# Where a feed-forward's temporary sums lie, and when the next weight is prepared

## The chip, the cores and the metric

The kernel runs on one core of a Trainium2 chip. The metric is the device time of one execution in microseconds. TensorE (PE) multiplies, ScalarE (ACT) and VectorE (DVE) prepare operands and read results back, GpSimd (POOL) and SyncE (SP) start transfers. Each engine works through its own list of instructions in order, and semaphores hold an instruction until what it needs is there. The lists are fixed when the kernel is built.

## The reference

Two layers of a decoder trunk on 512 tokens of width 1024, in float32. In each layer:

```python
h = rmsnorm(x)
z = h @ w_in                     # queries, keys, values of three token mixers, merge gates
m = sum(sigmoid(gate_b) * (mixer_b(z) @ w_br_b) for b in "abc")   # window, sparse, latent attention
x = x + m @ w_out
x = x + cross_attention(rmsnorm(x), rmsnorm(mem))    # 4 heads on 256 memory tokens, w_xq, w_xkv, w_xo
h = rmsnorm(x)
x = x + (silu(h @ w_gate) * (h @ w_up)) @ w_down     # 22 blocks of 128 hidden features
```

Mixer C is the latent attention: its queries come from a normalised latent of 384 features, by a product without and one with a rotary position, and its keys and values from a normalised latent of 256.

## The kernel before

**Numbers.** A float32 product is made of three matmuls: operand and weight are each split into a high half (a rounding cast on ScalarE) and a low half (the difference, on VectorE), and TensorE adds high x high, high x low, and low x high. In the code these are the matmuls of L307, L308 and L309 of `mm3`, or of L294 of `quads`. L307 and L308 need a weight's high half `wh` and the operand's two halves, L309 the weight's low half `wl`.

**Weights.** They stream through a fixed plan of units of 128 x 1024. `unit` takes the next one for a task. `load` starts its DMA on SyncE's queue (L222, three buffers `wraw`), and `halve` casts it (`wh`, L246, two buffers) and subtracts (`wl`, L166 by a helper). `ahead` loads further and prepares the next unit. `mm3` calls it after the block of 128 rows whose number is its argument `ahead`; with None it doesn't.

**Tiles that share a unit.** Four places use one unit for two tiles of output: the position projection of mixer C (`pe`, weight `w_mpe`, three blocks for each tile), its keys and values (`kv`, `w_mkv`), the merge product (`product`, `w_br`), and the output projection of the cross attention (`out_task`, `w_xo`). There the first tile passes None, and the second prepares the next unit.

**The order.** Tasks are Python generators that run side by side in stages (`skew`). A list scheduler then places each engine's instructions, so that the written order is not the order on an engine.

**The feed-forward.** The 22 pairs of gate and up blocks are computed in two ways. Pairs 0 to 3 are plain: `gate(j)`, `up(j)`. Pairs 4 to 21 use a scheme with seven products in place of eight: `p1` to `p7`, each of 12 matmuls of 256 columns (`quads`), in the order p1(4), p5(4), p2(4), p6(4), p3(4), p1(5), p7(4), p5(5), p2(5), p4(4), p6(5), p3(5), p1(6), p7(5). They need sums of weights and sums of operands.

- Sums of weights: `load_sum` copies the up block into a tile `sum` (tag S31r, two buffers, L262, SyncE) and adds the gate block to it by an accumulating DMA from GpSimd's queue (L266). `halve_sum` makes the halves `S31h` (L172) and `S31l` (L173), and then the tile is read once more for the sum `S24`.
- Sums of operands: `normed` makes the normalised operand `y` in the row form during `gate(1)` and `up(1)`. `sums(0)` follows `gate(2)` and `sums(1)` follows `up(2)`. Each makes four temporaries f[0] to f[3] from quarters of `y` and splits them into the tiles `T`, which the pair tasks read: `trans(i)` hands out T's part i, of which `p5`, `p6`, `p7` and `p4` read 0, 1, 2 and 3. f[1] is made from f[0], f[3] from f[1]. `operand` splits `y` itself into `xh` and `xl` for `p1`, `p2` and `p3`.

Before the change the four temporaries come from `self.tmp()`, a tag of five buffers that evacuated products use as well. The sums of pairs 4 and 5 are both loaded ahead of the feed-forward, since S31r's two buffers are free.

Of the kernel before, what the change touches and what calls it, by code (L numbers as in the profile page):

```python
# [8 lines left out]
F32 = mybir.dt.float32  # L9
# [137 lines left out]
class Trunk:  # L147
# [787 lines left out]
    def pe_tasks(self, l, lq, out):  # L935

        nc, w = self.nc, []

        def pe(t):
            if t == 0:  # L940
                w.append(self.unit("w_mpe", l, nblk=6))
            ps = self.mm()
            yield from self.mm3(ps, w[0], range(3 * t, 3 * t + 3), lq, ahead=1 if t else None)
            yield STAGE
            f, s = self.tmp(), self.tmp()
            nc.scalar.copy(f, ps)
            for q in range(0, 128, 32):
                nc.sync.dma_start(s[q:q + 16], f[q + 16:q + 32])
                nc.sync.dma_start(s[q + 16:q + 32], f[q:q + 16])
            yield STAGE  # L950
            yield 0
            yield STAGE
            r = self.pp.tile([128, 512], F32, name="lf", tag="lf", bufs=5)
            self.tt(s, s, self.spe, OP.mult)
            self.tt(r, f, self.cpe, OP.mult)
            self.tt(r, r, s, OP.add)
            out.append(r)

        return [pe(0), pe(1)]

    def pair_tasks(self, l, p, lq, lkv, pe, box):

        nc, at = self.nc, self.at
        w, fs, ks, vs = [], [], {}, {}

        def kv(g):
            if g == 0:
                w.append(self.unit("w_mkv", l, p, nblk=4))
            ps = self.mm()
            yield from self.mm3(ps, w[0], range(2 * g, 2 + 2 * g), lkv, ahead=0 if g else None)  # L970
            yield STAGE
            f = self.tmp()
            nc.scalar.copy(f, ps)
            yield STAGE
            tp = self.tp4(f)
            yield 430
            k = ks[g] = at.tile([128, 2, 512], F32R, name="k", tag="k", bufs=2)
            for i in range(2):
                nc.sync.dma_start(k[64:96, i].bitcast(F32), self.kpe[64 + 32 * i:96 + 32 * i].bitcast(F32))
            self.split(k[0:64, 0], k[0:64, 1], f[0:64])  # L980
            yield STAGE
            v = vs[g] = at.tile([128, 4, 128], F32R, name="v", tag="v", bufs=2)
            self.split(v[:, :, 64 * g:64 * g + 64], v[:, :, 64 - 64 * g:128 - 64 * g], tp[:, :, 64:128])

        def product():
            ps = yield from self.proj(("w_mq", l, p), lq)
            yield STAGE
            for g in range(2):
                f = self.tmp()
                h = 2 * p + g  # L990
                nc.scalar.copy(f[0:64], ps[64 * g:64 * g + 64])
                nc.scalar.copy(f[64:96], pe[h // 4][32 * (h % 4):32 * (h % 4) + 32])
                fs.append(f)

        def query(g):
            yield 0
            yield STAGE
            q = at.tile([128, 2, 512], F32R, name="q", tag="q", bufs=2)
            self.split(q[0:96, 0], q[0:96, 1], fs[g][0:96])
            yield STAGE  # L1000
            box[2 * p + g] = (q, ks[g], vs[g])

        return [kv(0), kv(1), product(), query(0), query(1)]

    def jobs_c(self, box, of):
# [27 lines left out]
    def merge_tasks(self, l, x, n, br, of, done=None):  # L1033

        nc = self.nc
        os, ts, ws = [], {}, {}

        def halves():
            yield 0
            for f in of:  # L1040
                o = self.mx.tile([128, 2, 512], F32R, name="oh", tag="oh", bufs=4)
                self.split(o[:, 0], o[:, 1], f)
                os.append((o[:, 0], o[:, 1]))
            del of[:]

        def gate(i):
            ps = yield from self.proj(("w_in", l, (T_GA, T_GB, T_GC)[br] + i), x)
            yield STAGE
            f = self.mx.tile([128, 512], F32, name="gt", tag="gt", bufs=2)
            self.evac(ps, n["r"], f)  # L1050
            nc.scalar.activation(f, f, AF.Tanh, scale=0.5)
            ts[i] = f

        def product(i):
            if i % 2 == 0:
                ws[i // 2] = self.unit("w_br", l, br, i // 2)
            w = ws[i // 2]
            b0 = 4 * (i % 2)
            ps = self.mm()
            yield from self.mm3(ps, w, range(b0, b0 + 4), os, ahead=1 if i % 2 else None)  # L1060
            yield STAGE
            t = ts.pop(i)
            if br == 0:
                m = self.mx.tile([128, 512], F32, name="mg", tag="mg", bufs=8)
                self.mg.append(m)
                nc.vector.scalar_tensor_tensor(m, t, 1.0, ps, op0=OP.add, op1=OP.mult)
            else:
                m = self.mg[i]
                nc.vector.scalar_tensor_tensor(t, t, 1.0, ps, op0=OP.add, op1=OP.mult)
                self.tt(m, m, t, OP.add)  # L1070
            if done is not None:
                yield STAGE
                done(m)

        out = [halves()]
        for i in range(0, 8, 2):
            out += [gate(i), gate(i + 1), product(i), product(i + 1)]
        return out
# [143 lines left out]
    def cross(self, l, st, xt, xa, mem):  # L1222
        nc = self.nc
        self.at = xa
        x, n, qs, os = st["x"], {}, {}, {}
# [42 lines left out]
        o = [(os[h][:, 0], os[h][:, 1]) for h in range(4)]  # L1268
        st, n = self.norm_begin(), {}
        ws = {}  # L1270

        def out_task(i):
            if i % 2 == 0:
                ws[i // 2] = self.unit("w_xo", l, i // 2)
            ps = self.mm()
            b0 = 4 * (i % 2)
            yield from self.mm3(ps, ws[i // 2], range(b0, b0 + 4), o, ahead=1 if i % 2 else None)
            yield STAGE
            self.tt(xt[i], xt[i], ps, OP.add)
            self.norm_split(st, xt[i], i, l * G_LAYER + G_FFN)  # L1280
            self.norm_tile(st, xt[i])

        drain(skew([out_task(i) for i in range(KT)]))
        return st, n

    def ffn(self, l, st, n, xt, ff, last):
# [39 lines left out]
        def sums(i):  # L1326

            if i == 0:
                ts.extend([[ff.tile([128, 4, 256], F32R, name="T", tag="T", bufs=8) for _ in "hl"] for _ in range(4)])
            c, f = slice(2 * i, 2 * i + 2), [self.tmp((128, 2, 256)) for _ in range(4)]  # L1330
            b11, b12, b21, b22 = (ys[k][:, :, h] for k in (i, 2 + i) for h in (slice(0, 256), slice(256, 512)))
            self.tt(f[0], b11, b12, OP.subtract)
            self.tt(f[2], b22, b12, OP.subtract)
            nc.vector.scalar_tensor_tensor(f[1], f[0], -1.0, b22, op0=OP.mult, op1=OP.subtract)
            nc.vector.scalar_tensor_tensor(f[3], f[1], -1.0, b21, op0=OP.mult, op1=OP.subtract)
            for t, src in zip(ts, f):
                self.split(t[0][:, c], t[1][:, c], src)
# [89 lines left out]
        def down(i, part):  # L1427
# [4 lines left out]
            if end:  # L1432
                if not last:
# [5 lines left out]
        m = sum(FFN_PARTS) - 1  # L1439
        tasks = [self.norm_end(st, D, n), gate(0), up(0), after(gate(1), (normed, 0), (normed, 2)),  # L1440
                 after(up(1), (normed, 1), (normed, 3)), after(gate(2), (sums, 0)), after(up(2), (sums, 1))]
        tasks += [gate(3), up(3)]
        for j in range(PLAIN, m):
# [12 lines left out]
        ws, sh, rh = {}, [self.norm_begin(256, nc.vector, ff) for _ in range(2)], [{}, {}]  # L1456
# [162 lines left out]
```

## Time and profile before

| | us |
|---|---|
| median of 3 runs | 2002.15 |
| lowest, highest | 2000.5, 2004.52 |
| the profiled execution | 2001.81 |
| its span in the trace | 2000.1 |
| TensorE busy in it | 1965.3 (98%) |
| VectorE busy | 1400.3 (70%) |
| ScalarE busy | 1187.7 (59%) |
| GpSimd busy | 70.1 (4%) |

The span runs from the first to the last instruction on the engines; what lies around it is 1.7 us. TensorE's busy time holds stretches in which several matmuls overlap in the pipeline, so gaps in the row of matmuls are read from the distance between their starts. In the names of the trace the buffer numbers are left out: `wh` is the same as `wh_6838` in the order below.

### The profile page before, as it was taken

What the parts mean: (1) busy time and instruction counts of PE and PEld (TensorE: products, weight loads), DVE (VectorE), ACT (ScalarE), POOL (GpSimd) and SP (SyncE); (2) the same over time, 40 slices, a digit from 0 to 9 for tenths busy, and PEclk for the clock granted to TensorE, in tenths of its full rate; (3) what the DMA queues carried; (4) which work ended last, traced back from release to release, by engine and by line L of the source; (5) the groups of instructions that cost most, each with busy time, mean ns of one, the idle gap of its engine ahead of it and who ended that gap; (6) DMA issues with size and microseconds to landing.
All of it is one profiled execution on the core that took longest, in us unless ns stands there. A gap on an engine that the chain in (4) does not pass through costs nothing.

```text
span 2000.1 us, 30439 instructions
## 1 busy us (share of the span) xinstructions
PE 1965.3 (98%) x11390; PEld 1691.0 (85%) x11390; DVE 1400.3 (70%) x2699; ACT 1187.7 (59%) x2282; POOL 70.1 (4%) x113
## 2 busy tenths in 40 slices
PE   8999999999999999999999999999999999999998
PEld 6878887888888798989878788878888888989898
DVE  7897777676557884847678877676665679657475
ACT  5777776875446552534456867877744566435254
POOL 1000000000000010100001000000000000001000
PEclk9999999999999999999999999999999999999999
DMA  6432212224332473645344322132333344657432
GB/s 193 116 91 60 68 48 82 77 88 139 100 105 87 129 200 116 184 123 137 112 133 110 83 68 59 55 90 74 116 111 106 99 132 114 167 141 196 115 104 73
DMA packets 86764, 220.07 MB, mean 110 GB/s; under 512 B 11208, under 2 KB 17096, under 8 KB 86616
## 3 DMA queue, kind: packets, MB, share of 16 engines
q1 hardware_dynamic: 76680, 199.21, 32.5%
q0 software_dynamic: 9792, 18.88, 5.9%
q8 instruction: 89, 1.46, 0.3%
q14 instruction: 59, 0.48, 0.1%
q10 hardware_dynamic: 144, 0.04, 0.0%
HBM read 200.23 MB, written 4.75 MB: 102 GB/s over the span
## 4 chain that ended last, share of the span: by engine, by line
PE 80%; DVE 8%; ACT 7%; DMA 2%; issue 2%; SPq 0%; POOL 0%; DVEq 0%; ACTq 0%
PE mm L307 17%; PE mm L309 17%; PE mm L308 17%; PE s L294 10%; PE tp L294 5%; PE av L674 3%; PE tp L628 3%; PE av L294 3%; ACT p L614 2%; ACT p L602 1%; DVE wl L166 1%; DMA sum<-in_w_gu 1%; ACT wh L246 1%; DVE p L596 1%; ACT ph L172 1%
## 5 line engine op out<-in xcount | busy, mean ns | idle before, releaser
L246 ACT CAST wh<-wraw 128x1024 fp32r<-128x1024 f32 (+3 forms) x275 | 277.5, 1009 | 397.0 <-PE mm L308 230.0
L307 PE MATMUL mm<-xh,wh 128*128 128x512 f32 x928 | 376.9, 406 | 3.4 <-ACT wh L246 2.0
L309 PE MATMUL mm<-xh,wl 128*128 128x512 f32 x928 | 366.0, 395 | 4.8 <-DVE wl L166 4.7
L166 DVE TENSOR_TENSOR wl<-wraw,wh 128x1024 fp32r<-128x1024 f32 (+3 forms) x275 | 322.7, 1174 | 64.2 <-ACT wh L246 61.2
L308 PE MATMUL mm<-xl,wh 128*128 128x512 f32 x928 | 367.1, 396 | 0.3 <-DVE xl L176 0.3
L309 PEld LDWEIGHTS mm<-xh,wl 128*128 128x128 f32 x928 | 174.8, 188 | 42.9 <-DVE wl L166 6.5
L307 PEld LDWEIGHTS mm<-xh,wh 128*128 128x128 f32 x928 | 175.3, 189 | 34.3 <-ACT wh L246 3.3
L308 PEld LDWEIGHTS mm<-xl,wh 128*128 128x128 f32 x928 | 175.6, 189 | 31.5 <-issue 1.7
L602 ACT ACTIVATE p<-p,st 128x256 f32<-128x256 f32 (+5 forms) x288 | 154.8, 538 | 57.2 <-DVE st L596 53.0
L166 DVE TENSOR_TENSOR x<-x,mm 128x512 f32<-128x512 f32 (+1 forms) x88 | 55.6, 637 | 146.0 <-PE mm L309 145.6
L614 ACT ACTIVATE p<-p,st 128x256 f32<-128x256 f32 (+3 forms) x288 | 139.9, 531 | 25.0 <-DVE st L166 16.5
L173 DVE TENSOR_TENSOR pl<-tp,ph 128x384 fp32r<-128x384 f32 (+1 forms) x192 | 116.7, 610 | 42.5 <-ACT ph L172 41.6
L596 DVE CUSTOM_DVE_ANT_0 p<-s,causal 128x128 f32<-128x128 f32 (+2 forms) x224 | 106.0, 475 | 43.3 <-PE s L1016 21.3
L172 ACT CAST ph<-tp 128x384 fp32r<-128x384 f32 (+1 forms) x192 | 98.7, 517 | 37.1 <-PE tp L628 35.1
L307 PE MATMUL mm<-h,wh 128*128 128x512 f32 x304 | 120.3, 396 | 0.0
L308 PE MATMUL mm<-h,wh 128*128 128x512 f32 x304 | 120.2, 395 | 0.0
L309 PE MATMUL mm<-h,wl 128*128 128x512 f32 x304 | 120.2, 395 | 0.0
L628 PE MATMUL tp<-ident,p 128*128 128x128 f32 x656 | 110.9, 277 | 4.8 <-DVE v L173 2.2
L266 POOL DMA_DIRECT2D sum<-in_w_gu x36 | 43.3, 1213 | 1581.4 <-DVE acc L166 530.5
L628 PEld LDWEIGHTS tp<-ident,p 128*128 128x128 f32 x656 | 75.7, 140 | 22.0 <-ACT p L614 8.3
L307 PE MATMUL mm<-oh,wh 128*128 128x512 f32 x192 | 79.4, 413 | 0.0
L309 PE MATMUL mm<-oh,wl 128*128 128x512 f32 x192 | 76.7, 399 | 0.0
(300 smaller groups left out, 4796.1 us busy)
## 6 DMA issues: line engine op xcount, KB each, us to landing
wraw<-in_w_in SPq DMA_DIRECT2D x91, 512.0 KB, 3.6
wraw<-in_w_gu SPq DMA_DIRECT2D x52, 512.0 KB, 3.7
sum<-in_w_gu SPq DMA_DIRECT2D x36, 512.0 KB, 4.4
sum<-in_w_gu POOLq DMA_DIRECT2D x36, 512.0 KB, 5.8
wraw<-in_w_d SPq DMA_DIRECT2D x32, 512.0 KB, 3.7
wraw<-in_w_br SPq DMA_DIRECT2D x24, 512.0 KB, 3.6
up<-in_w_gu SPq DMA_DIRECT2D x36, 256.0 KB, 3.4
wraw<-in_w_xkv SPq DMA_DIRECT2D x16, 512.0 KB, 3.6
```

What stands on the lines that cost most here:

```text
L166: (eng or self.nc.vector).tensor_tensor(out=out, in0=a, in1=b, op=op)
L172: nc.scalar.copy(hi, src)
L173: (eng or nc.vector).tensor_tensor(out=lo, in0=src, in1=hi.bitcast(F32), op=OP.subtract)
L246: nc.scalar.copy(wh[:, j:j + n], raw[:, j:j + n])
L294: nc.tensor.matmul(ps, a[:, c], b, start=start and i + k == 0, stop=i == 3 and k == 2, skip_group_check=not start)
L307: nc.tensor.matmul(ps, wh[:, c], xh, start=i == 0, stop=False)
L308: nc.tensor.matmul(ps, wh[:, c], xl, start=False, stop=False)
L309: nc.tensor.matmul(ps, wl[:, c], xh, start=False, stop=i == len(blocks) - 1)
L596: o.nc.vector.tensor_tensor_reduce(out=p, in0=self.ps.pop(i), in1=self.mask(self.blocks[i]), scale=-self.scale, scalar=self.init, op0=OP.a ...
L602: self.o.nc.scalar.activation(p, p, AF.Exp, scale=-1.0, bias=st[:, 0, i:i + 1], accum_out=st[:, 1, i:i + 1])
L614: nc.scalar.activation(self.p[j], self.p[j], AF.Copy, scale=self.st[:, 2, j:j + 1])
L628: o.nc.tensor.transpose(tp[:, n], self.p[j][:, c:c + 128], o.ident)
```

## The change

It has two parts. In the four places where two tiles share a unit, the first tile also prepares the next unit, after its block 0 or 1. And in `sums` the four temporaries no longer come from `tmp`, but from two tiles of the tag S31r, f[0] and f[1] in the first, f[2] and f[3] in the second. That tag has two buffers as before, so its tiles now follow each other in this order: the sum of pair 4, the temporaries of `sums(0)` (f_6994, f_6995), the sum of pair 5 (sum_7015), the temporaries of `sums(1)` (f_7056, f_7057), the sum of pair 6 (sum_7127), and so on. A tile can be written only when the last reader of the tile two places ahead of it is done.

```diff
-            yield from self.mm3(ps, w[0], range(3 * t, 3 * t + 3), lq, ahead=1 if t else None)
+            yield from self.mm3(ps, w[0], range(3 * t, 3 * t + 3), lq, ahead=1)
...
-            yield from self.mm3(ps, w[0], range(2 * g, 2 + 2 * g), lkv, ahead=0 if g else None)
+            yield from self.mm3(ps, w[0], range(2 * g, 2 + 2 * g), lkv, ahead=0)
...
-            yield from self.mm3(ps, w, range(b0, b0 + 4), os, ahead=1 if i % 2 else None)
+            yield from self.mm3(ps, w, range(b0, b0 + 4), os, ahead=1)
...
-            yield from self.mm3(ps, ws[i // 2], range(b0, b0 + 4), o, ahead=1 if i % 2 else None)
+            yield from self.mm3(ps, ws[i // 2], range(b0, b0 + 4), o, ahead=1)
...
-            c, f = slice(2 * i, 2 * i + 2), [self.tmp((128, 2, 256)) for _ in range(4)]
+            c, f = slice(2 * i, 2 * i + 2), []
+
+            for _ in range(2):
+                t = ff.tile([128, 2, 2, 256], F32, name="f", tag="S31r", bufs=2)
+                f += [t[:, 0], t[:, 1]]
```

What it does to the order is seen best on ScalarE. The first place is the start of mixer C in layer 0, where the latent `lat` is normalised (`rstd`, `lf`), the first keys and values (`tmp`) are copied out of PSUM, and `wraw_3553` is the unit of the merge product. Before:

```order
L375 COPY rstd_3544<-av_3542 128x512
L973 COPY tmp_3646<-mm_3623 128x512
L973 COPY tmp_3668<-mm_3633 128x512
L175 ACTIVATE lat_3578<-lf_3311,gains_69 128x512
L175 ACTIVATE lat_3582<-lf_3405,gains_69 128x512
L175 ACTIVATE lat_3586<-lf_3410,gains_69 128x512
L172 CAST k_3663<-tmp_3646 64x512
L246 CAST wh_3679<-wraw_3553 128x1024
```

After:

```order
L375 COPY rstd_3544<-av_3542 128x512
L973 COPY tmp_3646<-mm_3623 128x512
L246 CAST wh_3657<-wraw_3553 128x1024
L175 ACTIVATE lat_3578<-lf_3311,gains_69 128x512
L175 ACTIVATE lat_3582<-lf_3405,gains_69 128x512
L175 ACTIVATE lat_3586<-lf_3410,gains_69 128x512
L172 CAST k_3669<-tmp_3646 64x512
L973 COPY tmp_3674<-mm_3639 128x512
```

The cast of the merge product's weight (wh_3679 before, wh_3657 now) has moved from behind the latent to ahead of it, and the second copy from ahead of the latent to behind it. On VectorE the weight's subtraction has likewise moved ahead of the latent's three low halves, and on TensorE four of the eight transposes of the copies have moved behind the matmuls of the position projection. Layer 1 is the same.

The second place is the start of the feed-forward in layer 0: `S31h` are the sums of weights, `dh` a difference block for `p4`, `wh_6838` the weight of `up(1)`. Before:

```order
L364 ACTIVATE sd_6786<-av_6781,eps_71 128x4
L172 CAST S31h_7030<-sum_6956 128x1024
L172 CAST S31h_7159<-sum_7017 128x1024
L172 CAST dh_7192<-up_7020 128x512
L375 COPY rstd_6793<-av_6791 128x512
L246 CAST wh_6838<-wraw_6717 128x1024
L1299 ACT_TABLE_LOAD
L1299 ACTIVATE tmp_6826<-tmp_6826 128x512
```

After:

```order
L364 ACT_TABLE_LOAD
L364 ACTIVATE sd_6786<-av_6781,eps_71 128x4
L172 CAST S31h_7028<-sum_6956 128x1024
L375 COPY rstd_6793<-av_6791 128x512
L1299 ACT_TABLE_LOAD
L1299 ACTIVATE tmp_6826<-tmp_6826 128x512
L246 CAST wh_6838<-wraw_6696 128x1024
```

Only the sum of pair 4 is cast here now; `dh` has gone ahead of these rows, and the weight of `up(1)` stands behind the first SiLU (`tmp_6826`).

The third place is where the operand is split just ahead of the first pair task `p1(4)`. Before:

```order
L172 CAST xh0_6587<-y_6900 128x256
L172 CAST xh1_6607<-y_6900 128x256
L172 CAST xh2_6634<-y_6943 128x256
L172 CAST xh3_6655<-y_6943 128x256
L172 CAST T_6992<-tmp_7061 128x512
L172 CAST xh4_6682<-y_6903 128x512
L172 CAST xh5_6703<-y_6903 128x512
L172 CAST xh6_6730<-y_6946 128x512
L246 CAST wh_7134<-wraw_6959 128x1024
L172 CAST xh7_6738<-y_6946 128x512
```

After:

```order
L172 CAST xh0_6587<-y_6900 128x256
L172 CAST xh1_6613<-y_6900 128x256
L172 CAST S31h_7155<-sum_7015 128x1024
L172 CAST xh2_6634<-y_6943 128x256
L172 CAST xh3_6661<-y_6943 128x256
L172 CAST xh4_6682<-y_6903 128x512
L172 CAST xh5_6709<-y_6903 128x512
L172 CAST xh6_6730<-y_6946 128x512
L246 CAST wh_7130<-wraw_6959 128x1024
L172 CAST xh7_6738<-y_6946 128x512
```

The cast of the sum of pair 5 stands between xh1 and xh2 now. The two casts that made T from the second half's f[2] and f[3], of which `T_6992` stood in these rows, come some ten rows further on, behind the copy `s2` of `p6(4)`; on VectorE f_7057 is made behind the last of the low halves xl and behind the sums that read sum_7015. In SyncE's queue sum_7015 stands behind the unit `wraw_6959`, and sum_7127 two units further on.

## Rows read from the trace of the kernel before

Times are us from the start of the span.

**Rows 1.** The page: busy time of the engines, and the TensorE clock in 40 slices.

```profile
PE 1965.3 (98%) x11390; PEld 1691.0 (85%) x11390; DVE 1400.3 (70%) x2699; ACT 1187.7 (59%) x2282; POOL 70.1 (4%) x113
...
PEclk9999999999999999999999999999999999999999
```

**Rows 2.** TensorE's waits: us in total, times, longest us.

```profile
PE mm L309 <- DVE wl L166: 4.7, 3, 1.7
PE tp L530 <- ACT tmp L973: 2.3, 2, 1.2
```

**Rows 3.** TensorE timeline, layer 0, FFN start: start us, us, instruction, [idle, releaser].

```profile
667.71 0.39 PE L309 MATMUL mm<-xh,wl 128*128 128x512 f32 x1
669.32 0.49 PE L307 MATMUL mm<-xh,wh 128*128 128x512 f32 x1 [1.22 <-ACT wh L246]
669.65 0.40 PE L308 MATMUL mm<-xl,wh 128*128 128x512 f32 x1
671.56 0.50 PE L309 MATMUL mm<-xh,wl 128*128 128x512 f32 x1 [1.51 <-DVE wl L166]
```

**Rows 4.** The same of layer 1.

```profile
1654.57 0.40 PE L308 MATMUL mm<-xl,wh 128*128 128x512 f32 x1
1656.47 0.50 PE L309 MATMUL mm<-xh,wl 128*128 128x512 f32 x1 [1.51 <-DVE wl L166]
```

**Rows 5.** ScalarE timeline, layer 0, FFN start.

```profile
666.27 1.05 ACT L172 CAST S31h<-sum 128x1024 fp32r<-128x1024 f32 x1 [4.40 <-DMA sum<-in_w_gu]
...
668.22 1.05 ACT L246 CAST wh<-wraw 128x1024 fp32r<-128x1024 f32 x1
```

**Rows 6.** VectorE timeline, layer 0, FFN start and first pairs.

```profile
683.51 1.22 DVE L166 TENSOR_TENSOR wl<-wraw,wh 128x1024 fp32r<-128x1024 f32 x1
...
702.64 1.89 DVE L173 TENSOR_TENSOR xl<-y,xh 128x512 fp32r<-128x512 f32 x3
```

**Rows 7.** TensorE timeline, layer 0, start of mixer C.

```profile
330.17 1.15 PE L530 MATMUL tp<-ident,tmp 128*128 128x128 f32 x8 [1.16 <-ACT tmp L973]
331.41 0.74 PE L307 MATMUL mm<-lat,wh 128*128 128x512 f32 x2
332.27 0.50 PE L308 MATMUL mm<-lat,wh 128*128 128x512 f32 x1
```

**Rows 8.** ScalarE timeline, layer 0, start of mixer C.

```profile
329.52 1.08 ACT L973 COPY tmp<-mm 128x512 f32<-128x512 f32 x2
330.63 1.95 ACT L175 ACTIVATE lat<-lf,gains 128x512 fp32r<-128x512 f32 x3
...
332.99 1.05 ACT L246 CAST wh<-wraw 128x1024 fp32r<-128x1024 f32 x1
```

**Rows 9.** VectorE timeline, layer 0, start of mixer C.

```profile
329.66 1.90 DVE L166 TENSOR_TENSOR lf<-lf,rstd 128x512 f32<-128x512 f32 x3 [0.37 <-ACT rstd L375]
331.47 2.07 DVE L176 SCALAR_TENSOR_TENSOR lat<-lf,gains,lat 128x512 fp32r<-128x512 f32 x3
```

**Rows 10.** TensorE timeline, layer 0, first pair tasks.

```profile
698.43 0.28 PE L294 MATMUL s<-xh,wh 128*128 128x256 f32 x1
...
698.91 0.40 PE L294 MATMUL tp<-T,S31h 128*128 128x256 f32 x2
699.43 0.38 PE L294 MATMUL s<-xl,wh 128*128 128x256 f32 x1
```

**Rows 11.** Windows view, pair tasks: length, busy us (count) of PE, PEld, DVE, ACT, POOL.

```profile
715.00:730.00 15.00, 15.00 (x128) 15.00 (x127) 14.03 (x23) 9.63 (x15) 1.72 (x2) 1.00 0.92 238
```

**Rows 12.** SyncE's queue, layer 0: the sums' first DMA.

```profile
699.07 0.38 SPq L262 DMA_DIRECT2D sum<-in_w_gu  x1
```

**Rows 13.** GpSimd's timeline, layer 0: the sums' accumulating DMA.

```profile
702.99 1.18 POOL L266 DMA_DIRECT2D sum<-in_w_gu  x1 [45.77 <-DVE S24l L173]
```

**Rows 14.** The page, DMA issues: times, KB each, median us to landing.

```profile
sum<-in_w_gu POOLq DMA_DIRECT2D x36, 512.0 KB, 5.8
```

**Rows 15.** The tile sum, both its DMAs, 640 to 760 us.

```profile
DMA to landing us min/median/max: 3.4/5.9/10.6
```

## The prediction

> **What bounds the kernel now.** I read the page first. TensorE is busy for 98% of the span, and its granted clock stands at the upper level, 2.4 GHz, in all 40 slices [rows 1]. So TensorE is the bound, and a change that adds no matmul can only move its few gaps. The change adds none. The second view is the list of TensorE's waits: one wait is for a weight's low half from VectorE, 4.7 us in 3 cases, and one is for a copy ahead of the transposes of mixer C, 2.3 us in 2 cases [rows 2]. Third, I went to the timelines at each place where the two programs' order differs: the start of mixer C, the start of the FFN and its first pair tasks, once in each layer. Elsewhere the order of TensorE, ScalarE and VectorE is the same, or moved by an instruction where nothing waits (the output projection of the cross attention, the merges, the start of mixer B). I price those at nothing; the cover is TensorE's own backlog there, and the bound is 0.3 us either way.
>
> The sum is made against the profiled execution, 2001.81 us (span 2000.1). The median of the runs shown is 2002.15, so 0.34 us above it, which is less than the rounding of what follows.
>
> **Term 1, the FFN start: a stall goes.** Before, ScalarE casts both sums of pairs 4 and 5 ahead of the weight of `up(1)`. The second cast sat 4.40 us waiting for its DMA and began at 666.27; the weight's cast came at 668.22 [rows 5]. TensorE shows what that costs. Consecutive matmuls of 512 columns start 0.23 us apart when nothing waits. From 667.71 to 669.32 is 1.61, so 1.38 lost; from 669.65 to 671.56 is 1.91, so 1.68 lost [rows 3]. In layer 1 only the second gap is there: 1654.57 to 1656.47, 1.67 lost [rows 4]. Together 4.73 us. After the change the second sum's buffer holds the temporaries, its load comes later, and the order has that cast no longer ahead of `wh_6838`. What is late next? That cast now stands behind the SiLU of the first gate, which needs rstd, and rstd needs only TensorE's sum of squares. By the order I place its start some 1.5 us before the matmuls need it. I take the whole gain, **-4.7**. The other bound is that the low half, now behind two more VectorE operations, is late again by up to the same 1.68 in each layer: then -1.4.
>
> A small companion: the first pair task waited 0.28 us for an operand's low half (the matmul at 698.91 is doubled, so the next was due at 699.15 and came at 699.43) [rows 10]. Its VectorE rows now come earlier, as the sum's additions are placed ahead of them. Twice 0.28 is **-0.6**; the other bound is nothing.
>
> **Term 2, the first pair tasks: stalls appear.** A pair task is 12 matmuls of 256 columns. In 15.00 us TensorE did 128 of them [rows 11], 0.117 us each, so a task takes 1.41 us. Let P be the start of `p1(4)`, 698.43 before [rows 10]. Three things are chained through the two S31r buffers.
>
> (A) The load of `sum_7015` (pair 5) may begin once VectorE has read `f_6994` for the last time. In the order those are the weight's low half at 683.51, which takes 1.22, and then three operations of 512 columns at about 0.6 (three of the operand's take 1.89 [rows 6]): 683.51 + 1.22 + 1.8 is 686.5, or P - 11.9. The first DMA plus GpSimd's pickup took from 699.07 [rows 12] to 702.99 [rows 13], 3.9 us. The accumulating DMA took a median of 5.8 to land [rows 14]. So the sum is there at P - 2.2. ScalarE has its cast between the operand's casts `xh1` and `xh2`, and these were made just ahead of P. The cast starts late, and `xh2` to `xh7`, with the next weight's cast of 1.05 among them, move back with it. `xl7` comes out at about P + 3.8 to P + 4.7. `p2(4)` wants it 2 tasks and 10 matmuls after P, at about P + 4.0 less what TensorE can take out of turn. I take 0.6 us, with bounds of 0 and 1.3.
>
> (B) The second half's `f_7057` shares the buffer of `sum_7015`, so it waits until that sum has been cast and added to. Its low half in T is used in the third block of `p7(4)`, six tasks after P: at 6 x 1.41 + 0.7, P + 9.2. VectorE has, after `xl7`, eight rows at 0.4 to 1.2 us each ahead of it, and comes out at about P + 10.1. That is 0.9 us, with bounds of 0.3 and 1.2.
>
> (C) `f_7056` is read for the last time in that chain, so `sum_7127` (pair 6) goes out at about P + 9.5 and is there 3.9 + 5.8 later, at P + 19.2. ScalarE has its cast, 1.05 us, ahead of the copy `s2` that frees the bank for `p7(5)`, the 14th task, due at P + 18.4 plus A and B, or P + 19.9. The copy is done at about P + 20.7. I take 0.8 us, with bounds of 0 and 1.5.
>
> After these the order is that of before again, and VectorE catches up. 0.6 + 0.9 + 0.8 is 2.3 us in a layer, **+4.6** in two; bounds +0.6 and +8.0.
>
> **Term 3, the start of mixer C: a weight goes ahead of the latent.** TensorE stands for 1.16 us there already, waiting for the copy [rows 7], and the same 1.2 in the other layer [rows 2]. Before, ScalarE did two copies from 329.52, and then the high half of the latent from 330.63 [rows 8]; VectorE scaled three rows from 329.66 and started the low halves at 331.47 [rows 9]; the matmul that needs the first low half started at 332.27 [rows 7]. Now the weight of the merge product is prepared under the first tile of the position projection. Its cast, 1.05 us by the row at 332.99 [rows 8], stands between the two copies' places, and the second copy (0.54) goes behind the latent. The high half is 0.5 us later, which is hidden behind one row of VectorE. But VectorE has the weight's subtraction ahead of the low halves, 1.2 as in [rows 6]. So the L308 matmul of the latent starts 1.2 us later, and nothing that TensorE has in its order there fills it. Also, four of the eight transposes that filled the gap before now come after the projection's matmuls: half of the 1.15 us of that row is 0.57, and I take 0.45, since some of the row is waiting for the second copy. 1.65 in each layer, **+3.3**. Bounds: 0.5 in each layer if only the transposes move, 2.0 if both engines' delays add: +1.0 to +4.0.
>
> **The sum.** 2001.81 - 4.7 - 0.6 + 4.6 + 3.3 = **2004.4 us**. With all bounds on one side it would be 1998.1 (-4.7 - 0.6 + 0.6 + 1.0) or 2012.4.
>
> **The rule on the other side.** The tile of sums shows DMAs that landed in 3.4 us at best, 5.9 in the median and 10.6 at worst [rows 15]. The Trainium skill, DMA: Bandwidth & Descriptors, section Anatomy of one DMA, SWDGE path, gives about 2.0 us plus the bytes over 436 GB/s for such a transfer, an estimate of 3.2 us for these 512 KB. The trace has 5.8 for it, so the measurement decides. By the page's figure A and C would vanish.
>
> **Rivals.** *The sums land early.* If with the lighter traffic of this stretch the accumulating DMA takes the 3.4 of [rows 15] and not 5.8, every sum is there 2.4 us sooner, more than the 0.6 of A and the 0.8 of C. B stays, since VectorE sets it. Then 2004.4 - 2.8 is 2001.6: no change. For it: the transfer's own bytes are no more than a weight's. Against it: the median is that of 36 cases.
>
> *All that is lost is hidden, the gain stays.* TensorE has other work ready at mixer C and in the pairs, and only the lower bounds remain: about 1998, faster by 0.2%. Against it: at both places TensorE stood idle before already, for want of exactly this ready work [rows 3, 7].
>
> *The accumulating DMAs collide with the weights* (slower). The pairs run at a DMA share of 0.92 (the last number but one of [rows 11]), and the worst landing was 10.6 [rows 15], 4.8 above the median. ScalarE works in order, so its cast of the sum, and with it the operand's casts behind it, waits for as long as the DMA does. Each us beyond 5.8 costs nearly a us at A and again at C. Half of the 4.8 at both gives 2.4 x 2 x 2 = 9.6, or 2014; at 0.5 us beyond, 2006.4, it decides.
>
> *The low half stays late at the FFN start* (the change doesn't do what it says): 2004.4 + 3.3 = 2007.7.
>
> **How the numbers follow.** I take 0.2%, 4.0 us, as about what a measurement tells from no change. My forecast (2002 to 2006) gets 0.56, the early sums 0.14, the hidden loss 0.08, the collision 0.17, the late low half 0.05. Faster by more than 0.2% (below 1998.1) takes most of the hidden loss: 0.07. Slower (above 2006.2) takes the collision, all but 0.03, and the late low half, and a little of the forecast's upper side: 0.21. Same: 0.72. The range from 1998.5 to 2008.0 leaves out half of the hidden loss and most of the collision, 0.15.
>
> **What the changed profile would show.** Term 1: in TensorE's timeline no gap at the start of `up(1)`, and "mm L309 <- DVE wl" shorter by some 3 us; wrong if it is still there. Term 2: new gaps of 0.5 to 1 us within 22 us of the first 256-column matmul, released by VectorE (`xl`, `T`) and by ScalarE (`s`), with ScalarE idle for the sum's DMA ahead of them. Term 3: at the start of mixer C a gap ahead of L308 of about 1 us for `lat` from VectorE, and four transposes behind the projection. The forecast is wrong if ScalarE's wait for the sum's DMA exceeds 1 us, or if the latent's matmuls start when they did.

## The result and the profile after

The changed kernel took 2013.22 us (median of five runs) against 2001.33 for the kernel before, run beside it: 1.0059 times, with a 95% interval of 1.0049 to 1.007. A sixth run of it, at a mean granted clock of 0.65 in place of 0.996, took 2717.31 us and is not counted. It is 11.9 us slower; 2004.4 was forecast, and the range ended at 2008. The profiled execution took 2012.89 us, its span 2011.2, 11.1 more than before.

TensorE's list of waits shows both the gain and the losses (us in total, times, longest):

```profile
PE s L294 <- ACT s L1357: 2.4, 2, 1.5
PE tp L530 <- ACT tmp L973: 2.3, 2, 1.2
PE s L294 <- DVE tmp L166: 2.3, 2, 1.2
PE av L294 <- DVE xl L173: 2.2, 2, 1.1
PE mm L307 <- ACT lat L175: 2.1, 2, 1.0
...
PE mm L309 <- DVE wl L166: 1.7, 1, 1.7
...
PE mm L308 <- DVE lat L176: 1.6, 2, 0.8
PE s L294 <- DVE T L173: 1.3, 2, 0.6
...
PE s L294 <- ACT xh L172: 0.5, 1, 0.5
```

The wait for a weight's low half has shrunk from 4.7 us in 3 cases [rows 2] to 1.7 in one, which stands at the start of the kernel (25.63 us), and the wait for a weight's high half at the FFN start is gone. But there are seven waits that the list of before did not have: on the copy `s`, on `tmp`, on `xl`, `T` and `xh` in the pairs, on the two halves of `lat` in mixer C.

To see where the time went I compared, matmul by matmul counted from the start, when each was due in the two traces. The distance grows and shrinks mainly at eight places:

| stretch | layer 0 | layer 1 | both | forecast |
|---|---|---|---|---|
| up to and with mixer B | +0.44 | -0.07 | +0.4 | 0 |
| mixer C | +1.95 | +3.47 | +5.4 | +3.3 |
| FFN start, `up(1)` | -3.30 | -1.90 | -5.2 | -4.7 |
| first pair tasks | +5.44 | +5.02 | +10.5 | +4.0 (+4.6 - 0.6) |
| all | +4.53 | +6.52 | +11.1 | +2.6 |

The first pairs of layer 0 in TensorE's timeline; the first row is the start of `p1(4)`, the time that the prediction called P:

```profile
697.51 0.28 PE L294 MATMUL s<-xh,wh 128*128 128x256 f32 x1
...
698.84 0.39 PE L294 MATMUL s<-xh,wh 128*128 128x256 f32 x1 [0.46 <-ACT xh L172]
...
703.93 0.39 PE L294 MATMUL av<-xl,wh 128*128 128x256 f32 x1 [1.12 <-DVE xl L173]
...
710.22 0.39 PE L294 MATMUL s<-T,S31h 128*128 128x256 f32 x1 [0.65 <-DVE T L173]
...
720.56 0.50 PE L294 MATMUL s<-T,S31h 128*128 128x256 f32 x2 [0.91 <-ACT s L1357]
...
730.56 0.39 PE L294 MATMUL s<-xh,wh 128*128 128x256 f32 x1 [1.15 <-DVE tmp L166]
```

Counted as the distance between starts beyond the usual one, as in [rows 10], the five waits are 0.95 (0.61 at 698.84 and 0.34 at the next), 1.27, 0.81, 1.07 and 1.31 us, 5.41 together. The kernel before had 0.28 there [rows 10]; the rest of the 5.44 is that the matmul behind each wait comes about 0.1 us late too. In layer 1 the last four are 1.27, 0.80, 1.64 and 1.31, and the first is not there.

What released them is seen from SyncE's queue back to ScalarE. The two loads of sums, for pair 5 and pair 6, in SyncE's queue:

```profile
686.35 0.38 SPq L262 DMA_DIRECT2D sum<-in_w_gu  x1
...
709.02 0.38 SPq L262 DMA_DIRECT2D sum<-in_w_gu  x1
```

GpSimd's accumulating DMAs on the same two tiles:

```profile
690.73 1.21 POOL L266 DMA_DIRECT2D sum<-in_w_gu  x1 [31.86 <-DVE tmp L1310]
713.46 1.18 POOL L266 DMA_DIRECT2D sum<-in_w_gu  x1 [21.52 <-DVE wl L166]
```

ScalarE's casts of them, and what it does next:

```profile
697.44 1.05 ACT L172 CAST S31h<-sum 128x1024 fp32r<-128x1024 f32 x1 [2.76 <-DMA sum<-in_w_gu]
...
719.19 1.05 ACT L172 CAST S31h<-sum 128x1024 fp32r<-128x1024 f32 x1 [3.18 <-DMA sum<-in_w_gu]
720.14 0.37 ACT L1357 COPY s<-s 128x256 f32<-128x256 f32 x1
```

Pair 5's sum goes out at 686.35, GpSimd adds to it from 690.73, and the cast begins at 697.44: 11.1 us from the first issue. ScalarE stood for 2.76 us ahead of it, and the operand's casts `xh2` to `xh7` stood behind it. Pair 6 repeats this: out at 709.02, cast at 719.19, after 3.18 us of standing. VectorE, which had worked for 14.03 of 15 us in such a stretch before [rows 11], stands too, for the low half of that same sum:

```profile
716.68 0.42 DVE L166 TENSOR_TENSOR tmp<-s,tmp 128x256 f32<-128x256 f32 x1
720.27 1.23 DVE L173 TENSOR_TENSOR S31l<-sum,S31h 128x1024 fp32r<-128x1024 f32 x1 [3.17 <-ACT S31h L172]
```

Mixer C in layer 0: TensorE, and then ScalarE and VectorE.

```profile
330.63 0.66 PE L530 MATMUL tp<-ident,tmp 128*128 128x128 f32 x4 [1.16 <-ACT tmp L973]
332.32 0.73 PE L307 MATMUL mm<-lat,wh 128*128 128x512 f32 x2 [1.04 <-ACT lat L175]
333.87 0.50 PE L308 MATMUL mm<-lat,wh 128*128 128x512 f32 x1 [0.81 <-DVE lat L176]
```

```profile
329.98 0.59 ACT L973 COPY tmp<-mm 128x512 f32<-128x512 f32 x1
330.60 1.05 ACT L246 CAST wh<-wraw 128x1024 fp32r<-128x1024 f32 x1
331.55 1.94 ACT L175 ACTIVATE lat<-lf,gains 128x512 fp32r<-128x512 f32 x3
```

```profile
331.93 1.22 DVE L166 TENSOR_TENSOR wl<-wraw,wh 128x1024 fp32r<-128x1024 f32 x1
333.07 2.07 DVE L176 SCALAR_TENSOR_TENSOR lat<-lf,gains,lat 128x512 fp32r<-128x512 f32 x3
```

The weight's cast at 330.60 pushes the latent from 330.63 [rows 8] to 331.55, and the weight's subtraction pushes the low halves from 331.47 [rows 9] to 333.07 (the kernel runs 0.46 us behind that of before here). Beyond the first gap, which both kernels have, TensorE now loses 1.21 ahead of L307 and 0.97 ahead of L308, where it had lost 0.25 and 0.29. That is 1.64 us more (the remaining 0.3 of the 1.95 comes in small pieces behind these rows), and layer 1 has the same three waits to 0.01 us. It nevertheless lost 1.5 us more, and the granted clock says why (windows: length, busy us of PE, PEld, DVE, ACT, POOL, then clock, DMA share, GB/s; the first is layer 0):

```profile
334.00:336.00 2.00, 2.00 (x9) 1.60 (x10) 2.00 (x5) 1.27 (x4) 0.00 (x0) 1.00 0.39 133
1320.00:1322.50 2.50, 0.66 (x4) 0.42 (x4) 2.13 (x5) 2.48 (x5) 0.00 (x0) 1.00 0.80 239
1322.50:1324.10 1.60, 0.73 (x2) 0.30 (x2) 1.60 (x3) 1.60 (x4) 0.00 (x0) 1.00 0.47 118
1325.50:1327.00 1.50, 1.50 (x5) 1.13 (x5) 1.43 (x3) 0.04 (x1) 0.00 (x0) 0.50 0.01 4
1328.70:1331.00 2.30, 2.30 (x14) 1.89 (x13) 0.97 (x2) 1.28 (x3) 0.00 (x0) 1.00 0.24 52
```

Behind the waits of layer 0 TensorE runs at the upper level. Behind those of layer 1 it runs at the lower one, 1.2 GHz, for some 3.4 us, with matmuls 0.43 us apart in place of 0.23, before it comes back. The profile's page does not show this: its row of the clock has a 9, for 90% or more, in every slice of 50 us, as in [rows 1].

### The profile page after: what moved, and what is told of

The parts are those of the page before. It is cut to its first block, busy times and chain, and to the rows that moved or that the text cites. A ratio compares the mean times of both kernels' runs of the same rounds, so it can differ in the third digit from the quotient of the medians.

```text
span 2011.2 us, 30436 instructions
## 1 busy us (share of the span) xinstructions
PE 1968.9 (98%) x11390; PEld 1692.2 (84%) x11390; DVE 1400.2 (70%) x2699; ACT 1188.6 (59%) x2282; POOL 70.0 (3%) x113
## 4 chain that ended last, share of the span: by engine, by line
PE 76%; DVE 11%; ACT 7%; DMA 3%; issue 2%; SPq 0%; DVEq 0%; ACTq 0%; POOLq 0%
PE mm L307 16%; PE mm L309 16%; PE mm L308 16%; PE s L294 9%; PE tp L294 4%; PE av L674 3%; PE tp L628 3%; DMA sum<-in_w_gu 2%; PE av L294 2%; DVE wl L166 2%; DVE tmp L166 1%; ACT p L602 1%; ACT p L614 1%; DVE p L596 1%; ACT wh L246 1%
## 5 line engine op out<-in xcount | busy, mean ns | idle before, releaser
L307 PE MATMUL mm<-xh,wh 128*128 128x512 f32 x928 | 376.6, 406 | 1.9 <-ACT xh L175 1.2
L308 PE MATMUL mm<-xl,wh 128*128 128x512 f32 x928 | 367.3, 396 | 0.3 <-DVE xl L176 0.3
L307 PEld LDWEIGHTS mm<-xh,wh 128*128 128x128 f32 x928 | 175.3, 189 | 32.3 <-ACT xh L175 1.8
L308 PEld LDWEIGHTS mm<-xl,wh 128*128 128x128 f32 x928 | 175.5, 189 | 31.5 <-issue 1.7
L307 PE MATMUL mm<-h,wh 128*128 128x512 f32 x304 | 120.3, 396 | 0.0
L308 PE MATMUL mm<-h,wh 128*128 128x512 f32 x304 | 120.2, 395 | 0.0
L266 POOL DMA_DIRECT2D sum<-in_w_gu x36 | 43.2, 1201 | 1592.7 <-PE mm L308 533.4
L307 PE MATMUL mm<-oh,wh 128*128 128x512 f32 x192 | 79.6, 414 | 0.0
```

The costliest lines, as they stand in the source:

```text
L307: nc.tensor.matmul(ps, wh[:, c], xh, start=i == 0, stop=False)
L308: nc.tensor.matmul(ps, wh[:, c], xl, start=False, stop=False)
```

## The experiments

All are built from the kernel before. "Before" stands for the runs of that kernel on the same chip in the same job: 2001.81 for the first four, 2001.43 for the next three, 2002.52 for the last two. Where runs of different jobs are compared, the difference of their distances from their own "before" is given too.

**e1: only the temporaries.** The part of the diff in `sums`, without the four others.

> Only the temporaries move to S31r; no first tile prepares a weight. Theory (the sums of weights arrive late): the FFN keeps what the changed kernel showed, -3.3 and -1.9 us at its start, +5.4 and +5.0 in the first pairs, so 5.2 us slower than before (about 2006.6). Rival 1 (the weights prepared early disturb the FFN's loads, and cause its loss): about 5 us faster than before. Rival 2 (the sums' lateness came only of the 2 us that mixer C had lost): between.

Measured: 2007.21, 1.0028 times before (1.0017 to 1.004), so 5.4 us slower. Its trace has the FFN starts at -3.3 and -1.9, and the pairs at +5.1 and +5.3, with the same waits as above within 0.5 us. So the move to S31r alone makes the stalls, without help from mixer C or the early weights.

**e2: only the early weights.** The four lines with `ahead`, and the temporaries in `tmp`.

> Only the first tiles prepare the next weight; the temporaries stay in tmp. Theory: mixer C loses 2.0 us in layer 0 and 2.0 to 3.5 in layer 1 (the difference is whether TensorE's granted clock falls there), mixer B 0.4, the FFN nothing: 4.4 to 5.9 us slower than before, 2005.7 to 2007.2. Rival: the early weights cost the FFN as well, 10 us or more.

Measured: 2014.41, 1.006 times before (1.0048 to 1.0073), 12.6 us slower. The theory is refuted; the rival had the size, but only in part the cause. Mixer C cost 4.2 us or more in each layer, with the same three waits as above and the clock at the lower level behind them both times:

```profile
335.50:337.50 2.00, 2.00 (x6) 1.56 (x5) 0.36 (x2) 0.59 (x1) 0.00 (x0) 0.50 0.00 0
1327.50:1330.50 3.00, 3.00 (x9) 2.32 (x8) 1.36 (x4) 0.59 (x1) 0.00 (x0) 0.50 0.00 0
```

And the FFN starts cost 2.6 more than before in layer 0 and 0.5 in layer 1, though the order there is that of before.

**e3: the early weights without that of `pe`.**

```diff
-            yield from self.mm3(ps, w[0], range(3 * t, 3 * t + 3), lq, ahead=1)
+            yield from self.mm3(ps, w[0], range(3 * t, 3 * t + 3), lq, ahead=1 if t else None)
```

> As the run with only the weights prepared early, but without it in the position projection pe. Theory: the whole loss of mixer C comes from that one place, so the time of before within 0.6 us. Rival: keys and values, merge product and cross attention have a part in it, 1 us or more slower than before.

Measured: 2006.68, 1.0023 times before (1.0013 to 1.0033), 4.9 us slower, in nine runs from 2002.79 to 2011.12. Half of the theory holds: mixer C costs nothing here, so its whole loss belongs to `pe`; the time is the rival's. But 3.9 us came at the FFN start of layer 0, in TensorE's timeline:

```profile
670.09 0.49 PE L307 MATMUL mm<-xh,wh 128*128 128x512 f32 x1 [2.39 <-ACT wh L246]
...
672.33 0.79 PE L309 MATMUL mm<-xh,wl 128*128 128x512 f32 x1 [1.51 <-DVE wl L166]
```

and in the windows there:

```profile
668.00:672.00 4.00, 0.73 (x2) 0.30 (x2) 3.88 (x5) 3.94 (x6) 0.00 (x0) 0.91 0.10 11
672.00:676.00 4.00, 3.67 (x9) 2.90 (x10) 3.98 (x7) 1.57 (x2) 0.00 (x0) 0.50 0.56 185
```

It is the stall of [rows 3], 1.2 us longer in this run since pair 5's sum landed later. Then the clock is at the lower level for about 6 us, which takes another 2.7. So 1.2 us more of waiting for a DMA's landing cost 3.9 us. `e2` had the same in layer 0: 1.0 more of waiting, and 1.6 at the lower level.

**e4: only the first half in S31r.**

```diff
+            if i == 0:
+                for _ in range(2):
+                    t = ff.tile([128, 2, 2, 256], F32, name="f", tag="S31r", bufs=2)
+                    f += [t[:, 0], t[:, 1]]
+            else:
+                f = [self.tmp((128, 2, 256)) for _ in range(4)]
```

> No early weights; the temporaries of sums(0) lie in S31r, those of sums(1) in tmp. Theory: pair 5's sum is as late as before this edit and costs 1.2 us or less in a layer (A), but the wait of f_7057 (B) and the late sum of pair 6 (C, D) go; with the 5.2 gained at the FFN start that is 2.8 us faster than before, about 1998.5. Rival (VectorE is too full in the pairs, whatever the sums do): 2 us slower than before or more.

Measured: 1997.19, 0.9976 times before (0.9968 to 0.9985). It is 4.6 us faster, more than expected. The waits on `T`, on `s` and the last one on `tmp` are gone, and the pairs cost 1.1 and 0.5 us. Pair 6's sum is now loaded right behind pair 5's, where in the changed kernel it went out at 709.02:

```profile
683.41 2.18 SPq L262 DMA_DIRECT2D sum<-in_w_gu  x2
```

Most of what is left is on ScalarE, in layer 0:

```profile
691.75 1.02 ACT L172 CAST xh<-y 128x256 fp32r<-128x256 f32 x3
695.81 1.05 ACT L172 CAST S31h<-sum 128x1024 fp32r<-128x1024 f32 x1 [3.04 <-DMA sum<-in_w_gu]
696.77 2.48 ACT L172 CAST xh<-y 128x256 fp32r<-128x256 f32 x5
```

Three operand casts, then 3.04 us of standing for the sum's DMA, and then the other five.

**e5: without the accumulating DMA.** e1 without this line of `load_sum`:

```diff
-        nc.gpsimd.dma_start(s, ends, accum_op=OP.add)
```

> As the run with only the temporaries moved (2007.2, 5.4 us slower than before), but the accumulating DMA of the sums is left out, so that a sum of weights holds the up block alone and is there when SyncE's DMA has landed. The buffers and the temporaries stay in S31r. Theory (the loss comes of sums that land late): the stalls of 1.3, 0.8, 1.1 to 1.5 and 1.3 us in the first pairs go, in both layers, and the time is 4 to 5.5 us below before, 1996.5 to 1998. Rival (VectorE's moved work and the shared buffers cost it, whenever the sums land): 2004 or more.

Measured: 1995.18, 0.9962 times before (0.9949 to 0.9976), and no wait over 0.1 us in the first pairs of either layer. ScalarE casts the same two sums:

```profile
685.84 1.05 ACT L172 CAST S31h<-sum 128x1024 fp32r<-128x1024 f32 x1 [0.65 <-DMA sum<-in_w_gu]
...
706.47 1.05 ACT L172 CAST S31h<-sum 128x1024 fp32r<-128x1024 f32 x1 [1.44 <-DMA sum<-in_w_gu]
```

The buffers, the temporaries and VectorE's work on them are those of e1. The landing is earlier, and with it the order on ScalarE and VectorE: e1's casts of these sums began at 693.06 and 714.89, 7.2 and 8.4 us later. Some 12 us went (11.7 by the distances from "before"). The edit takes away the accumulating DMA of all 36 sums, so alone it doesn't tell the lateness of two sums from the traffic and GpSimd's work of all. `e4` does: it keeps every accumulating DMA, brings pair 6's sum forward, and loses the waits behind it. With both, the stalls are the lateness of the sums. B went too: `f_7057` waited for `sum_7015`, and so for the same DMA.

**e7: another pairing of the temporaries.** e4 with this line added:

```diff
+                f = [f[0], f[2], f[1], f[3]]
```

> As e4, but f[0] and f[2] share the first tile, f[1] and f[3] the second. By the order, ScalarE's cast of pair 5's sum then comes behind all casts of the operand, not between xh2 and xh3. Theory: the 0.9 and 0.65 us that e4 still lost there (an operand's casts waiting behind a sum's DMA) go, so 0.5 to 1.6 us below e4's 1997.2. Rival (those waits come from VectorE's load): the same as e4.

Measured: 1995.74, 0.9966 times before (0.9953 to 0.9978), 1.45 below e4 (1.1 by the distances from "before"), as the theory had it. The intervals of the two overlap, but the traces agree: the pairs, which cost e4 1.1 and 0.5 us, are 0.3 faster than before in each layer. It is the fastest kernel here that computes the whole. The cast of the sum comes behind all the operand's casts now, and the DMA is there by then:

```profile
691.29 1.32 ACT L172 CAST xh<-y 128x256 fp32r<-128x256 f32 x4
...
693.04 2.18 ACT L172 CAST xh<-y 128x512 fp32r<-128x512 f32 x4
...
696.08 1.05 ACT L172 CAST S31h<-sum 128x1024 fp32r<-128x1024 f32 x1
```

The load itself goes out no earlier than in e4, but 1.8 us later, so that it is the place of the cast that helps:

```profile
685.23 0.38 SPq L262 DMA_DIRECT2D sum<-in_w_gu  x1
```

**e8: e4 with the early weights of e3.**

> e4 with the three early weights of e3 (keys and values, merge product, cross attention). e3 was 4.9 us slower than before, and its trace showed 3.9 of it at the FFN start of layer 0, where a stall that the kernel before has too grew by 1.2 us and the granted clock then fell to half. Theory: e8 has no stall there, so it is within 1 us of e4, plus 0.8 at mixer B: 1997.2 to 1999. Rival (the three early weights cost it wherever they stand): 4 us or more above e4.

Measured: 1999.62, 0.9989 times before (0.998 to 0.9998), 2.4 above e4 (2.8 by the distances from "before"): between the theories. The FFN start has no stall and cost nothing, as the theory said. In its trace 0.4 came at mixer B of layer 0, 0.2 behind mixer C in each layer, and 2.4 (1.1 in e4) at the first pairs of layer 0, where `xl` and `tmp` were late by 1.4 and 0.8; layer 1 doesn't show it. Both are late sums again: pair 5's load went out 1.3 us later than in e4, at 684.67, and an accumulating DMA issued at 719.56 took 9.4 us, for which VectorE stood 2.27 us ahead of that `tmp`. Why they were later in layer 0 alone stays open. So the three early weights cost 2 to 3 us even where no stall of the FFN start is left, and they gained nothing.

**e9: e7 with the early weight of `pe` alone; e10: e9 with filler.** e10 adds:

```diff
+            for _ in range(6 if t == 0 else 0):
+                nc.tensor.matmul(ps, w[0][0][:, :128], w[0][0][:, :512], start=True, stop=True)
```

> e7 with one early weight, that of the position projection pe. It has no other stall near the places where the clock fell. Theory: mixer C costs 1.9 us in a layer where the granted clock stays up, and 3.5 to 4.2 where it falls, so 3.8 to 8.4 us above e7 (1999.5 to 2004). Rival (the loss belongs to kv, product or out_task): the same as e7.

> e9 with six extra matmuls of 512 columns, 0.23 us each, on data that is long there; their result is overwritten. In TensorE's order they stand between the sum of squares and the transposes, where it idles for 1.3 us, so that they cost 0.1 us at most in a layer. Theory (the clock falls because TensorE has stood idle for too much of that stretch): it stays at the upper level in both layers, and e10 is 3.8 us above e7, with no part for the clock, up to 4.4 below e9. Rival (the fall comes of something else, such as the load of the other engines): e10 is the same as e9, or 0.2 above.

Measured: e9 2001.87, 6.1 above e7 (5.0 by the distances from "before"), as expected (1.0 times before, 0.9991 to 1.0009). In its trace mixer C costs 1.8 us in layer 0 and 3.3 in layer 1. e10 2000.91, 1.0 below e9 (0.999, 0.9981 to 0.9999): inconclusive. e9's windows just behind the waits, layer 0 and layer 1:

```profile
332.00:334.00 2.00, 1.99 (x9) 1.59 (x10) 2.00 (x4) 1.42 (x4) 0.00 (x0) 1.00 0.50 133
1316.00:1318.00 2.00, 1.72 (x4) 1.43 (x5) 2.00 (x4) 1.69 (x4) 0.00 (x0) 0.56 0.42 136
```

e10's:

```profile
332.00:334.00 2.00, 2.00 (x6) 1.54 (x7) 2.00 (x4) 1.31 (x4) 0.00 (x0) 0.61 0.51 131
1318.00:1320.00 2.00, 2.00 (x10) 1.58 (x9) 2.00 (x5) 1.24 (x4) 0.00 (x0) 1.00 0.48 125
```

The filler does stand in the gap. In TensorE's timeline of layer 0 the six matmuls run right up to the transposes:

```profile
326.94 1.96 PE L944 MATMUL mm<-wh 128*128 128x512 f32 x6
328.73 0.60 PE L530 MATMUL tp<-ident,tmp 128*128 128x128 f32 x4
```

That took away the 1.33 us that TensorE stands in the other kernels, and left the waits of 1.2 and 0.97. Yet the clock fell in layer 0 and not in layer 1, the other way round from e9. So the theory that the clock stays up without the first gap is refuted as it was put. What decides between the levels, with the same waits ahead, stays open.

## Why the prediction was wrong, step by step

**Term 1 was right.** -4.7 was forecast, and the two FFN starts gave -5.2: the waits were counted to 0.01 us, but not that the matmul behind each comes about 0.1 us late as well. The cast for `up(1)` moved ahead of the wait for pair 5's sum. The small companion, -0.6, belongs to the first pairs; in layer 1 it came, and in layer 0 the wait for `xl` stayed, as a part of A.

**Term 2 failed, and it carries most of the miss**: +4.6 forecast, +10.4 of waits measured, beyond the bound of +8.0. The chain was the right one, A, B and C stood where they were put, and B was right in size (0.81 and 0.80 for 0.9). Its cause was not: the prediction had B stay when the sums land early, and in e5 it went. The forecast is 5.8 short: 2.3 at A, 1.1 at C and 2.6 at a fifth stall that was put at nothing, less 0.2 at B. Two steps were wrong.

- *The landing.* "So the sum is there at P - 2.2." The issue came at P - 11.2 (P is 697.51), near the P - 11.9 put down. But the DMA to the tile with GpSimd's pickup took 4.4 us, not 3.9, and the accumulating one 6.7 to the cast, not 5.8. The sum was there at about P, and ScalarE stood 2.76 us for it, where the prediction had called itself wrong above 1 us. A became 2.2 us in layer 0 (0.95 and 1.27) and 1.3 in layer 1, where 0.6 was taken. For pair 6 the accumulating DMA took the 5.7 that was put down, but the issue was 2 us later (P + 11.5), about as much as A was too small by, and C became 1.07 and 1.64 for 0.8. Against the estimate of 3.2 us from the Trainium skill (DMA: Bandwidth & Descriptors, Anatomy of one DMA), the measurement went further to the other side.
- *"After these the order is that of before again, and VectorE catches up."* This step, which put everything behind C at nothing, had no row behind it, and it was false. The wait for pair 6's sum left VectorE idle for 3.17 us in a stretch where it has about 1 us in 15 to spare [rows 11]. What it lost came back to TensorE ten us later as a fifth stall, 1.31 us in each layer. e4, in which that wait is gone, and e5, in which it is 0.59 us, have no such stall.

The 5.8 was no middle value either. The accumulating DMA of line L266 by itself, all 36 of the kernel before:

```profile
DMA to landing us min/median/max: 5.6/5.8/10.9
```

The median lies just above the minimum, so the sum could well come later but hardly earlier. The 3.4 of [rows 15], on which the rival of the early sums stood, is the plain DMA's.

That the lateness was the cause, and not the buffers or VectorE's moved rows, is what e5 and e4 show: with the same buffers and an early landing all of it went, and with all the DMAs kept, the part behind the sum that was brought forward.

**Term 3 was right in its mechanism and, in layer 0, in its size.** 1.65 was worked out, and the waits grew by 1.64 in each layer. L308 comes 1.14 us later, for which 1.2 was taken; 0.46 of that stands ahead of L307 already, since the later high half was not hidden as forecast. e3 shows that all of it belongs to `pe`, and e9 that `pe` alone brings it. What was missing is the clock, which fell behind the waits of layer 1 and cost 1.5 us there; in e2 it fell in both. Nothing in the trace of before says that it would fall there: the clock stays up at both places, and is at 0.50 only near the start (25 to 31 us) and at the very end. But a bound of 4.0 that knew only waits was too low.

**The sum of parts does not add.** e1 and e2 alone are 5.4 and 12.6 us slower, and together 11.9. The stall that e2 makes worse at the FFN start is the one that the move of the temporaries takes away; and at mixer C the clock fell in both layers of e2's trace, and in one of the changed kernel's.

**The rivals.** The hidden loss, the early sums and the late low half are refuted by the traces above. (Against the hidden loss the prediction cited [rows 3] for the pairs; those rows are the FFN start, and in the pairs only the 0.28 of [rows 10] was shown.) The collision had the right sign, and its 2014 lies near the measured time, but that is luck: it needs accumulating DMAs that take 2.4 us longer at A and at C, and in layer 0 they took 0.9 longer at A and no longer at C. By its own price of a us for each, that is less than 2 us in both layers. The rest is the late issue and the chain behind C, which it lacked.

## What to carry to other kernels

A buffer that is lent to temporaries also decides when the next load into it can start. Price that load to its end, here two DMAs one behind the other and 11 us from issue to cast, and then ask what stands behind the instruction that waits for it: engines that work in order hand the wait on to everything behind. Lending it to the half that is done early, with a pairing that puts the cast of the late sum behind the operand's casts (e7), kept the whole gain at no cost. And VectorE, 94% busy here, did not catch up within the stretch: its idle time came back on the path.

## What the runs showed of the hardware

A stall of TensorE can cost more than its length. After waits of 1.33, 1.21 and 0.97 us at mixer C the granted clock went to the lower level (1.2 GHz) in five of eight cases: one of the changed kernel's two layers, both of e2's, one of e9's, and, with the first wait filled, one of e10's. In the seven traces without the early weight of `pe`, where these waits are 1.33, 0.25 and 0.29, it never fell there. Matmuls were then 0.43 us apart and not 0.23 for 3 to 7 us, at a price of 1.5 to 2.6 us. At the FFN start of layer 0 the clock stayed up in the kernel before, with 1.38 and 1.68 us of waiting; it fell in e2 with 2.41 and 1.68, and in e3 with 2.55 and 1.68, where it took 2.7. The same stretch of the same program fell in one layer and not in the other. The Trainium skill (TensorE: Matmul & The Clock Gate, Part 1) says that the activity is judged at moments that are not tied to the kernel's start; this would fit, but no run here tests it.
